# A streaming-encoder layer: two feature blocks half plain, their combinations on VectorE, taps on ScalarE, and a gate put into down weights

## The chip, the core and the metric

The kernel runs as one program on one core of a Trainium2 chip. The metric is the device time of a launch in microseconds; the table below gives three runs and one profiled execution. The engines are called TensorE (PE in the rows; PEld is its weight load), VectorE (DVE), ScalarE (ACT), GpSimd (POOL) and SyncE (SP, which issues nearly all transfers). All sums are in fp32; a matmul operand is split into a rounded part and a rest (hi and lo), and each product is three matmuls: hi x hi, hi x lo, lo x hi.

## What is computed

One layer of an encoder for 1024 prompt tokens and 8 x 16 sample tokens, 1152 in all. Ahead of the part in question lie the input projection, attention and retention. The rest, cut to what matters:

```python
x = x + gt_m * (mixed @ w_out)
h = rmsnorm(x, g_ffn) * (1.0 + sc_f) + sh_f
u = h @ w_up                                    # 1024 x 5632
ue = concatenate([conv_prev, u], axis=1)
y = sum(w_conv[j] * ue[:, j:j + L] for j in range(3)) + b_conv
a, g = split(y, 2)
x = x + gt_f * ((silu(a) * g) @ w_down)         # 2816 x 1024
y_out = rmsnorm(x, g_final)
```

`gt_f`, `sc_f` and `sh_f` come from a conditioning vector per sequence: one for the prompt, eight for the sample streams.

## The kernel before, in words

**Output projection** (`mains`, `merge`, `tail`). The tokens are nine tiles of 128, taken in the order 0, 4, 1, 5, 2, 6, 3, 7, 8; tile 8 holds the sample tokens. Each tile has two halves of 512 output columns, with weights of their own (`woh`, `wol`). `merge` multiplies by the gate on VectorE (`tm`) and adds x on GpSimd. `tail` norms the tile (`xn`), transposes it on TensorE (8 transposes), applies scale and shift on VectorE (`hfc`), stores it to the DRAM tensor `d_h`, and splits it into `hhi` and `hlo`, the matmul operands.

**Up projection** (`up`, one call for each of 22 feature blocks of 128 features `a` and 128 features `g`). The input is taken as 2 halves of h (kh) by 2 halves of the tokens (th, 576 each), and the product as seven products in place of eight, numbered 1 to 7, with combinations of weights (`up_first`, `up_rest`) and of tokens (`t_sets`: t5, t6, t7, and a combination that takes the place of part of `hhi`). A product is done in two chunks of 288 tokens (c = 0, 1), 12 matmuls each: 14 x 12 = 168 a block. Products 1, 6, 7 and 4 add up in one PSUM bank, which is read between them. `t_sets(c)` loads four pieces of `d_h` into buffers `y`, subtracts (VectorE and GpSimd, line 1223) and splits. It needs 576 tokens of each half, so all tiles of the order but, for c = 0, tiles 3, 7 and 8. In the kernel before, both sets are built behind the last `tail`.

`conv` makes the three taps of the width-3 convolution over the whole block row `U` on VectorE: one `tensor_scalar` (line 1263) and two `scalar_tensor_tensor` (line 1266); `a` then goes through SiLU on ScalarE, the two are multiplied (line 1329) and stored to `d_g`.

**Down projection.** The 22 blocks are taken in groups (`GROUPS`). For each group and each tile and half, TensorE sums the group's products into one bank; VectorE adds the bank to `facc` (line 1476). `entry` loads and splits the next group's rows of `d_g` and weights. In the group before the last ("pen"), `facc` is multiplied by the gate (line 1482) and x is added on GpSimd (line 1483); in the last group the sum of a bank is multiplied by the gate (line 1479) and added by GpSimd, or for tile 7 by VectorE (line 1480). `finish_rows` norms a tile and stores it.

**What sets the order.** TensorE's instructions stand in program order. A scheduler sets the order on the other engines; each engine then runs its list strictly in order, so an instruction that waits holds all behind it. SyncE's transfers are such a list too.

Of the kernel before, what the change touches and what calls it, by code (L numbers as in the profile page):

```python
# [15 lines left out]
D = 1024  # L16
# [23 lines left out]
GROUPS = (2, 4, 3, 4, 3, 3, 3)  # L40
# [7 lines left out]
def body(ctx: ExitStack, tc: tile.TileContext, i):  # L48
# [818 lines left out]
    def up_first(A, s1):  # L867
# [202 lines left out]
    with ExitStack() as st:  # L1070
        c2 = cp = st.enter_context(pool("cb"))
# [57 lines left out]
        def tail(t, xt):  # L1129
# [7 lines left out]
            for q in range(2):  # L1137
# [26 lines left out]
        for n in range(1, NT):  # L1164
# [23 lines left out]
        up_rest(A0, s10, W0)  # L1188
        tail(NT - 1, xs.pop(NT - 1))

    wo_st.close()
    tails = ctx.enter_context(pool("tl")).tile([128, 18, 44], F32, name="tails")
    fst = ExitStack()
    tx = fst.enter_context(pool("tx"))
    TT = {p: [tx.tile([128, 4, TH], F32R, name=f"t{p}{z_}") for z_ in "hl"] for p in (5, 6, 7)}
    fp = fst.enter_context(pool("f"))

    def ytile():
        return fp.tile([128, UW], F32, tag="y", bufs=4, name="y")
# [14 lines left out]
    def t_sets(c):  # L1214
# [15 lines left out]
        sub(G, b[0, 1], b[1, 1], b[0, 1])  # L1230
# [3 lines left out]
        sub(G, b[1, 0], b[1, 0], b[1, 1])  # L1234
        s4 = slice(TH + c * CW, TH + c * CW + CW)
        split(hhi[:, 0:4, s4], hlo[:, 0:4, s4], b[1, 0])

    def up(ft, W, order, mid=None):
        kts = [s_ * NFT + ft for s_ in range(2)]
        Us, ys, X, Y, p5 = [], {}, {}, {}, {}  # L1240
        for s_ in range(2):
            U = fp.tile([128, UW], F32, tag="U", bufs=2, name="U")
# [28 lines left out]
        def keep(s_):  # L1271
            G.tensor_copy(tails.rearrange("p (i j) k -> p i j k", j=2)[:, :, :, kts[s_]],
                          Us[s_][:, SEQ:].rearrange("p (i c) -> p i c", c=2)[:, 0::9])

        def post3(c):
            for o_, ps_ in second(0, c, Y[3, c]):
                V.tensor_tensor(out=o_, in0=o_, in1=ps_, op=ALU.add)

        nb_ = [0]
        seen = set()  # L1280
        for p, c in order:
# [4 lines left out]
            else:  # L1286
                Y[p, c] = bank(nb_[0] // 2)
                nb_[0] += 1
                o = Y[p, c][:, 0:CW]
# [7 lines left out]
            seen.add((p, c))  # L1297
# [285 lines left out]
```

## Time and profile before

| | us |
|---|---|
| three runs | 1600.34, 1606.54, 1608.24 (median 1606.54) |
| the profiled execution | 1601.77 |
| its span in the profile | 1599.9 |
| TensorE busy in it | 1524.6 |
| VectorE, ScalarE, GpSimd busy | 1019.3, 513.7, 421.5 |

A line of the profile gives an engine, a source line of the kernel, the operation, the tensor written and the tensors read, and shapes as partitions x elements. Times are microseconds unless marked ns. "idle before" is what the engine stood still ahead of an instruction, and the name behind the arrow is what ended it. PEclk is the granted clock of TensorE; 1.00 stands for 2.4 GHz and 0.5 for 1.2 GHz.

### The profile page before, as it was taken

What the parts mean: (1) busy time and instruction counts of PE and PEld (TensorE: products, weight loads), DVE (VectorE), ACT (ScalarE), POOL (GpSimd) and SP (SyncE); (2) the same over time, 40 slices, a digit from 0 to 9 for tenths busy, and PEclk for the clock granted to TensorE, in tenths of its full rate; (3) what the DMA queues carried; (4) which work ended last, traced back from release to release, by engine and by line L of the source; (5) the groups of instructions that cost most, each with busy time, mean ns of one, the idle gap of its engine ahead of it and who ended that gap; (6) DMA issues with size and microseconds to landing.
All of it is one profiled execution on the core that took longest, in us unless ns stands there. A gap on an engine that the chain in (4) does not pass through costs nothing.

```text
span 1599.9 us, 27087 instructions
## 1 busy us (share of the span) xinstructions
PE 1524.6 (95%) x10544; PEld 1382.9 (86%) x10544; DVE 1019.3 (64%) x1754; ACT 513.7 (32%) x1039; POOL 421.5 (26%) x443
## 2 busy tenths in 40 slices
PE   6999999999999999899679999999999999999996
PEld 5866999998998898788569999999999987888785
DVE  5711248888755335455687888888888865544456
ACT  5401125555322423332332333323333244212102
POOL 2000021210221004333344444444444310000065
PEclk9999999999999999999979999999999999999998
DMA  9865321213258477565422222222222236322022
GB/s 304 267 253 183 93 85 53 67 42 98 65 188 276 142 247 241 168 215 165 152 79 83 77 70 66 79 83 76 70 62 83 83 129 215 122 84 85 34 92 118
DMA packets 190315, 203.89 MB, mean 127 GB/s; under 512 B 11181, under 2 KB 149723, under 8 KB 190188
## 3 DMA queue, kind: packets, MB, share of 16 engines
q1 hardware_dynamic: 171212, 187.22, 36.1%
q10 hardware_dynamic: 18976, 14.95, 2.9%
q8 instruction: 83, 1.36, 0.4%
q14 instruction: 44, 0.36, 0.1%
HBM read 152.56 MB, written 49.56 MB: 126 GB/s over the span
## 4 chain that ended last, share of the span: by engine, by line
PE 81%; DVE 6%; DMA 5%; issue 3%; ACT 2%; SPq 1%; POOL 1%; POOLq 0%; ACTq 0%; DVEq 0%
PE dn L61 9%; PE dn L63 9%; PE dn L62 9%; PE pb L1295 6%; PE pb L1294 6%; PE pb L1296 6%; PE dn L1295 3%; PE dn L1296 3%; PE dn L1294 3%; PE pf L62 2%; PE pf L63 2%; PE pf L61 2%; PE tp L660 2%; PE sc L625 1%; PE pa L372 1%
## 5 line engine op out<-in xcount | busy, mean ns | idle before, releaser
L61 PE MATMUL dn<-w,hhi 128*128 128x256 f32 x648 | 190.6, 294 | 0.0
L63 PE MATMUL dn<-w,hlo 128*128 128x256 f32 x648 | 182.1, 281 | 0.0
L62 PE MATMUL dn<-w,hhi 128*128 128x256 f32 x648 | 181.8, 281 | 0.0
L1266 DVE SCALAR_TENSOR_TENSOR y<-U,cv,y 128x1168 f32<-128x1168 f32 x88 | 153.6, 1747 | 1.6
L61 PEld LDWEIGHTS dn<-w,hhi 128*128 128x128 f32 x648 | 123.0, 190 | 12.0 <-issue 10.2
L63 PEld LDWEIGHTS dn<-w,hlo 128*128 128x128 f32 x648 | 122.8, 190 | 7.5 <-issue 7.5
L62 PEld LDWEIGHTS dn<-w,hhi 128*128 128x128 f32 x648 | 123.0, 190 | 4.3 <-issue 4.2
L245 POOL TENSOR_TENSOR sg<-sg,rot 128x256 f32<-128x256 f32 x36 | 28.1, 782 | 275.1 <-DVE rot L244 233.6
L1483 POOL TENSOR_TENSOR facc<-facc,x 128x1024 f32<-128x1024 f32 x9 | 21.7, 2406 | 229.2 <-DVE facc L1482 229.2
L57 ACT CAST sl<-raw 128x512 fp32r<-128x512 f32 x66 | 39.0, 620 | 108.3 <-PE pb L1295 59.1
L57 ACT CAST se<-raw 128x512 fp32r<-128x512 f32 x66 | 41.1, 622 | 95.3 <-PE dn L1295 52.3
L61 PE MATMUL dn<-hhi,w 128*128 128x384 f32 x192 | 69.3, 361 | 0.0
L63 PE MATMUL dn<-hhi,w 128*128 128x384 f32 x192 | 64.6, 336 | 0.0
L62 PE MATMUL dn<-hlo,w 128*128 128x384 f32 x192 | 64.5, 336 | 0.0
L58 DVE TENSOR_TENSOR w<-raw,w 128x512 fp32r<-128x512 f32 x56 | 38.9, 709 | 37.3 <-ACT w L57 25.1
L878 POOL TENSOR_TENSOR raw<-s,raw 128x512 f32<-128x512 f32 x22 | 49.5, 2249 | 46.6 <-DVE se L58 46.5
L61 PE MATMUL dn<-woh,mh 128*128 128x512 f32 x144 | 58.7, 408 | 1.7 <-issue 1.2
L1294 PE MATMUL dn<-t5h,sl 128*128 128x288 f32 x168 | 51.1, 304 | 8.6 <-issue 5.6
L1295 PE MATMUL pb<-t6l,sl 128*128 128x288 f32 x176 | 53.4, 303 | 6.0 <-DVE t6l L58 6.0
L62 PE MATMUL dn<-wol,mh 128*128 128x512 f32 x144 | 56.9, 395 | 2.2 <-DVE wol L58 2.2
L1476 DVE TENSOR_TENSOR facc<-facc,pf 128x512 f32<-128x512 f32 x45 | 30.9, 686 | 43.4 <-PE pf L63 42.3
L631 ACT ACTIVATE e<-sc,sm 128x128 f32<-128x128 f32 (+7 forms) x64 | 47.4, 745 | 30.9 <-DVE sm L630 30.1
(395 smaller groups left out, 4979.1 us busy)
## 6 DMA issues: line engine op xcount, KB each, us to landing
wa<-in_w_ada SPq DMA_DIRECT2D x48, 512.0 KB
raw<-in_w_up SPq DMA_DIRECT2D x88, 256.0 KB
raw<-in_w_in SPq DMA_DIRECT2D x56, 256.0 KB
gr<-d_g SPq DMA_DIRECT2D x20, 576.0 KB
d_g<-y SPq DMA_DIRECT2D x22, 512.0 KB
wr<-in_w_down SPq DMA_DIRECT2D x40, 256.0 KB
kc<-in_cache_k SPq DMA_DIRECT2D x8, 1024.0 KB
vc<-in_cache_v SPq DMA_DIRECT2D x8, 1024.0 KB
```

What stands on the lines that cost most here:

```text
L57: S.copy(hi, src)
L58: V.tensor_tensor(out=lo, in0=src, in1=hi.bitcast(F32), op=ALU.subtract)
L61: T.matmul(out, lhsT=sh, rhs=mh, start=first, stop=False)
L62: T.matmul(out, lhsT=sh, rhs=ml, start=False, stop=False)
L63: T.matmul(out, lhsT=sl, rhs=mh, start=False, stop=last)
L631: S.activation(out=e[:, hf, 0:nk], in_=s_[:, 0:nk], func=ACTF.Exp, bias=sm[:, hf:hf + 1], scale=1.0, accum_out=sm[:, 2 + hf:3 + hf])
L660: T.matmul(po[:, 0:128], lhsT=pTs[n // 4][:, n % 4], rhs=vt[:, n], start=(n == 0), stop=(n == qb))
L878: G.tensor_tensor(out=A[0, 0], in0=s1, in1=A[0, 0], op=ALU.subtract)
L1266: V.scalar_tensor_tensor(out=y[:, j0:j1], in0=U[:, j0 + j:j1 + j], scalar=wconv[j][:, kt:kt + 1], in1=y[:, j0:j1], op0=ALU.mult, op1=ALU.add)
L1294: T.matmul(o, lhsT=sh, rhs=mh, start=st_, stop=False, skip_group_check=True)
L1295: T.matmul(o, lhsT=sh, rhs=ml, start=False, stop=False, skip_group_check=True)
L1296: T.matmul(o, lhsT=sl_, rhs=mh, start=False, stop=en, skip_group_check=True)
```

## The change

1. **Blocks 0 and 1 half plain** (`NPL = 2`). Chunk 0 goes as before, with seven products. Chunk 1 is done plain, as eight products (`block`, the entries "q" of the order): 96 matmuls in place of 84. These need no combination of tokens. `t_sets(1)` is called behind block 1.
2. **Hand-over.** In block 0, products 1 and 2 of chunk 0 and the first halves of both plain parts come first (72 matmuls); then `handover` calls the last `tail`, frees the projection's memory, and calls `t_sets(0)` and the weights of block 1.
3. **Combinations on VectorE.** All four of a block's weights, and all four of a token set.
4. **Taps on ScalarE.** The first tap, and the scale and shift of tiles 0 to 7 in `tail`.
5. **Last group.** The last tile of it, 8, is done inside the group before, with the weights as they are; then the last group's down weights are loaded again, multiplied by the prompt's gate and split, so that the bank's sum is simply added to `facc`. The groups are 2, 2, 4, 3, 4, 3, 4 in place of 2, 4, 3, 4, 3, 3, 3.

```diff
-GROUPS = (2, 4, 3, 4, 3, 3, 3)
+GROUPS = (2, 2, 4, 3, 4, 3, 4)
+NPL = 2
...
+        late(4, A[1, 1])
+        V.tensor_tensor(out=s1, in0=A[1, 0], in1=A[1, 1], op=ALU.add)
+        late(5, s1)
+        V.tensor_tensor(out=A[1, 0], in0=A[0, 0], in1=A[1, 0], op=ALU.subtract)
+        V.tensor_tensor(out=A[0, 0], in0=s1, in1=A[0, 0], op=ALU.subtract)
+        late(6, A[0, 0])
+        V.tensor_tensor(out=A[0, 1], in0=A[0, 1], in1=A[0, 0], op=ALU.subtract)
...
-                        V.tensor_scalar(out=hf_[:, kk], in0=p_[:, k], scalar1=A[:, kk, 0:1], scalar2=B[:, kk, 0:1],
-                                        op0=ALU.mult, op1=ALU.add)
+                        S.activation(out=hf_[:, kk], in_=p_[:, k], func=ACTF.Identity, scale=A[:, kk, 0:1],
+                                     bias=B[:, kk, 0:1])
...
-        sub(G, b[0, 1], b[1, 1], b[0, 1])
+        sub(V, b[0, 1], b[1, 1], b[0, 1])
...
-            V.tensor_scalar(out=y[:, j0:j1], in0=U[:, j0:j1], scalar1=wconv[0][:, kt:kt + 1],
-                            scalar2=bconv[:, kt:kt + 1], op0=ALU.mult, op1=ALU.add)
+            S.activation(out=y[:, j0:j1], in_=U[:, j0:j1], func=ACTF.Identity, scale=wconv[0][:, kt:kt + 1],
+                         bias=bconv[:, kt:kt + 1])
...
+    def handover():
+        tail(NT - 1, xs.pop(NT - 1))
+        cb_st.close()
+        wo_st.close()
...
+        t_sets(0)
+        late_["W"] = up_w(1)
...
-    t_sets(0)
-    t_sets(1)
-    W = up_w(1)
...
+    mixed = [(1, 0), (5, 0), (2, 0), ("q", 0), (6, 0), ("q", 1), (3, 0), ("q", 0), (7, 0), ("q", 1), (4, 0)]
+    up(0, W0, [(1, 0), (2, 0), ("q", 0), ("q", 1), ("q", 0), ("q", 1), (5, 0), (6, 0), (3, 0), (7, 0), (4, 0)],
+       (4, handover))
...
+            up(ft, W, mixed if ft < NPL else both)
+        if ft == NPL - 1:
+            t_sets(1)
...
+                if pen and n_ == 4:
+                    for hf in range(2):
+                        add(8, hf, sums(8, [ents[n] for n in range(starts[NG - 1], NFT)], hf))
+                    gated_rows(8)
+                    finish_rows(8, facc[8], gfin)
+                    for n in range(starts[NG - 1], NFT):
+                        for hf in range(2):
+                            sl = slice(hf * 512, hf * 512 + 512)
+                            raw = wraw()
+                            nc.sync.dma_start(raw, i["w_down"][n * 128:n * 128 + 128, sl])
+                            V.tensor_tensor(out=raw, in0=raw, in1=gts[0][:, sl], op=ALU.mult)
+                            split(*(z_[:, sl] for z_ in ents[n][1]), raw)
```

Two places of VectorE's list show what moves. The first is the end of the projection, from the last two products with the gate (`tm`) to the scale of tile 8 (`hfc` from `mA`); `y` is a piece of `d_h`, `sl` a weight's rest, `rstd` and `xn` the norm of tile 8. Before:

```order
L1121 TENSOR_TENSOR tm<-dn,gtm 128x512 x2
L1144 TENSOR_SCALAR hfc<-ct,mA_83,mB_85 128x128 x8
L58 TENSOR_TENSOR sl<-s_7932,sl 128x512
L130 TENSOR_SCALAR rstd<-ss 128x1
L58 TENSOR_TENSOR sl<-raw,sl 128x512
L1134 TENSOR_SCALAR xn<-xt,rstd 128x1024
```

And with the change:

```order
L1130 TENSOR_TENSOR tm<-dn,gtm 128x512
L1226 TENSOR_TENSOR y<-y 128x1152
L1130 TENSOR_TENSOR tm<-dn,gtm 128x512
L1226 TENSOR_TENSOR y<-y 128x1152 x2
L59 TENSOR_TENSOR hlo<-hfc,hhi 128x4x128
L1226 TENSOR_TENSOR y<-y 128x1152
L59 TENSOR_TENSOR sl<-raw,sl 128x512
L1338 TENSOR_TENSOR U<-U,dn 128x288
L131 TENSOR_SCALAR rstd<-ss 128x1
L59 TENSOR_TENSOR hlo<-hfc,hhi 128x4x128
L59 TENSOR_TENSOR sl<-s_7932,sl 128x512
L1143 TENSOR_SCALAR xn<-xt,rstd 128x1024
```

All four subtractions of the first token set, which used to stand behind tile 8, are now ahead of its norm, one of them ahead of its last product with the gate. Block 0's first results (`U`) are read there too.

The second is VectorE's list between blocks 1 and 2: block 1's second convolution (two L1271) and the second token set (L1226, then the rests t5l and t7l). With the change:

```order
L1271 SCALAR_TENSOR_TENSOR y<-U,cv,y 128x1168
L59 TENSOR_TENSOR sl<-raw,sl 128x512
L1271 SCALAR_TENSOR_TENSOR y<-U,cv,y 128x1168
L59 TENSOR_TENSOR se<-raw,se 128x512
L1226 TENSOR_TENSOR y<-y 128x1152
L1352 TENSOR_TENSOR y<-y 128x1024
L890 TENSOR_TENSOR raw<-s_9050,raw 128x512
L1226 TENSOR_TENSOR y<-y 128x1152
L1354 TENSOR_TENSOR y<-y 128x128
L59 TENSOR_TENSOR t5l<-y,t5h 128x4x288
L1226 TENSOR_TENSOR y<-y 128x1152
L59 TENSOR_TENSOR t7l<-y,t7h 128x4x288
```

The second set stands behind the convolution of block 1, and the product of block 1 (L1352, L1354) between its subtractions.

## Rows read from the trace of the kernel before

**Rows 1.** The page, part 2: busy tenths of TensorE in 40 slices of the span.
```profile
PE   6999999999999999899679999999999999999996
```
**Rows 2.** Windows: length; busy of PE, PEld, DVE, ACT, POOL; clock, DMA share, GB/s.
```profile
700.00:772.00 72.00, 72.00 (x346) 59.01 (x345) 38.85 (x83) 21.92 (x34) 23.33 (x22) 1.00 0.51 165
...
780.10:831.20 51.10, 31.98 (x171) 29.86 (x170) 40.54 (x51) 16.75 (x22) 21.91 (x15) 0.71 0.43 130
...
1000.00:1200.00 200.00, 200.00 (x1506) 199.78 (x1505) 172.04 (x231) 64.97 (x126) 94.78 (x90) 1.00 0.24 74
...
1320.00:1340.00 20.00, 17.61 (x67) 13.32 (x66) 13.47 (x17) 13.68 (x22) 0.00 (x0) 0.91 0.92 312
1340.00:1586.30 246.30, 246.21 (x1057) 196.78 (x1055) 129.78 (x170) 43.13 (x64) 44.53 (x30) 1.00 0.26 90
1586.30:1599.90 13.60, 0.00 (x0) 0.00 (x0) 7.71 (x10) 3.32 (x7) 3.30 (x6) 0.67 0.32 128
```
**Rows 3.** Waits of TensorE, 772 to 831.2 us: for whom, total, times, longest.
```profile
PE pb L1295 <- DVE t6l L58: 6.0, 2, 3.0
PE dn L1294 <- issue: 5.6, 1, 5.6
PE ct L1140 <- DVE xn L1134: 4.9, 1, 4.9
PE dn L1295 <- DVE t5l L58: 4.5, 2, 2.3
PE dn L1294 <- ACT t5h L57: 3.0, 1, 3.0
```
**Rows 4.** Timeline of VectorE around tile 8's tail: start, length, instruction.
```profile
767.29 0.69 DVE L1121 TENSOR_TENSOR tm<-dn,gtm 128x512 f32<-128x512 f32 x1 [0.83 <-PE dn L63]
772.79 0.69 DVE L1121 TENSOR_TENSOR tm<-dn,gtm 128x512 f32<-128x512 f32 x1 [4.80 <-PE dn L63]
...
777.67 0.75 DVE L1134 TENSOR_SCALAR xn<-xt,rstd 128x1024 f32<-128x1024 f32 x1
...
780.14 1.07 DVE L1148 TENSOR_TENSOR hfc<-ct,mA 128x128 f32<-128x128 f32 x5
...
793.69 1.36 DVE L1223 TENSOR_TENSOR y<-y 128x1152 f32<-128x1152 f32 x1 [1.01 <-DMA y<-d_h]
```
**Rows 5.** Timeline of TensorE between the projection and block 0.
```profile
772.59 1.03 PE L1140 MATMUL ct<-ident_all,xn 128*128 128x128 f32 x8
778.47 1.96 PE L1140 MATMUL ct<-ident_all,xn 128*128 128x128 f32 x8 [4.85 <-DVE xn L1134]
...
781.43 0.44 PE L1296 MATMUL pb<-hhi,se 128*128 128x288 f32 x1
781.67 0.41 PE L1294 MATMUL pb<-hhi,se 128*128 128x288 f32 x1
```
**Rows 6.** Timeline of SyncE: the loads of the first token set.
```profile
787.37 2.31 SPq L1219 DMA_DIRECT2D y<-d_h  x4
```
**Rows 7.** Groups of VectorE, 793 to 831 us: busy us, mean ns.
```profile
L58 DVE TENSOR_TENSOR t6l<-y,t6h 128x1152 fp32r<-128x1152 f32 x2 | 7.5, 3746 | 0.0
...
L1223 DVE TENSOR_TENSOR y<-y 128x1152 f32<-128x1152 f32 x4 | 5.4, 1349 | 1.0 <-DMA y<-d_h 1.0
L1266 DVE SCALAR_TENSOR_TENSOR y<-U,cv,y 128x1168 f32<-128x1168 f32 x2 | 2.9, 1430 | 0.0
```
**Rows 8.** Lines 1263 and 1269, all of the span: min/median/max ns, first and last start.
```profile
L1263 DVE TENSOR_SCALAR y<-U,cv x44: 875/880/1978, 824.9 to 1302.3; 128x1168 f32<-128x1168 f32 x44
...
L1269 ACT ACTIVATE y<-y x22: 1181/1182/1192, 829.0 to 1300.1; 128x1168 f32<-128x1168 f32 x22
```
**Rows 9.** Timeline of VectorE at the end.
```profile
1590.70 0.68 DVE L1479 TENSOR_TENSOR tm<-tp,gtf 128x512 f32<-128x512 f32 x1
...
1592.71 0.68 DVE L1480 TENSOR_TENSOR facc<-facc,tm 128x512 f32<-128x512 f32 x1
```
**Rows 10.** GpSimd in the group before the last, 1510 to 1550 us: busy us, mean ns.
```profile
L1483 POOL TENSOR_TENSOR facc<-facc,x 128x1024 f32<-128x1024 f32 x8 | 19.2, 2404 | 227.4 <-DVE facc L1482 227.4
```

More of the change, by code (lines that the diff above doesn't have):

```diff
@@ L1271, in keep, with done, block @@
         def keep(s_):
-            G.tensor_copy(tails.rearrange("p (i j) k -> p i j k", j=2)[:, :, :, kts[s_]],
+            G.tensor_copy(late_["tails"].rearrange("p (i j) k -> p i j k", j=2)[:, :, :, kts[s_]],
                           Us[s_][:, SEQ:].rearrange("p (i c) -> p i c", c=2)[:, 0::9])
[L1275 to L1281, printed above, removed]
+        def done(s_, th, c):
+            have.add((s_, th, c))
+            if th and c:
+                keep(s_)
+            if len([z_ for z_ in have if z_[0] == s_]) == 4:
+                conv(s_, 0, YW)
+        nb_ = nbank
+        have = set()
+        def block(s_, c):
+            for th in range(2):
+                o = bank(nb_[0] // 2)[:, 0:CW]
+                nb_[0] += 1
+                for kh in range(2):
+                    for k in range(4):
+                        cs = slice(th * TH + c * CW, th * TH + c * CW + CW)
+                        kk = kh * 4 + k
+                        mm3(o, *(z_[:, k] for z_ in W[((1, 2), (0, 4))[s_][kh]]), hhi[:, kk, cs], hlo[:, kk, cs],
+                            kk == 0, kk == 7)
+                if th:
+                    for o_, ps_ in second(s_, c, o):
+                        S.copy(o_, ps_)
+                else:
+                    S.copy(Us[s_][:, 2 + c * CW:2 + c * CW + CW], o)
+                done(s_, th, c)
+                yield
+        blocks = [block(s_, 1) for s_ in range(2)]
+        for n_, (p, c) in enumerate(order):
+            if mid and mid[0] == n_:
+                mid[1]()
+            if p == "q":
+                next(blocks[c])
+                continue
             if p in (1, 6, 7, 4):
@@ L1313, in up @@
                     V.tensor_tensor(out=o_, in0=ps_, in1=q_, op=ALU.add)
[L1314 to L1315 removed]
+                done(1, 1, c)
             elif p == 3:
[L1317 to L1318 removed]
+                for o_, ps_ in second(0, c, o):
+                    V.tensor_tensor(out=o_, in0=o_, in1=ps_, op=ALU.add)
+                done(0, 1, c)
             else:
                 S.copy(Us[1][:, f0], o)
[L1321 to L1327 removed]
+                done(1, 0, c)
         ya, yg = ys[0], ys[1]
@@ L1370, in body @@
         if last:
-            up(ft, W, [(p, c) for p in (1, 2, 5, 6, 3, 7, 4) for c in range(2)], ((3, 1), early))
+            up(ft, W, [(p, c) for p in (1, 2, 5, 6, 3, 7, 4) for c in range(2)], (10, early))
         else:
-            up(ft, W, both)
+            up(ft, W, mixed if ft < NPL else both)
+        if ft == NPL - 1:
+            t_sets(1)
         W = Wn
@@ L1448, in finish_rows, with sums, add, gated_rows @@
             nc.sync.dma_start(y_out, f)
-        for g in range(len(GROUPS)):
-            es = [ents.pop(n) for n in range(starts[g], starts[g + 1])]
-            pen, last = g == len(GROUPS) - 2, g == len(GROUPS) - 1
+        def sums(t, es, hf):
+            tk, sl = slice(t * 128, (t + 1) * 128), slice(hf * 512, hf * 512 + 512)
+            p_ = dbank()
+            for n, (g_, w_) in enumerate(es):
+                mm3(p_, g_[0][:, tk], g_[1][:, tk], w_[0][:, sl], w_[1][:, sl], n == 0, n == len(es) - 1)
+            return p_
+        def add(t, hf, p_):
+            sl = slice(hf * 512, hf * 512 + 512)
+            V.tensor_tensor(out=facc[t][:, sl], in0=facc[t][:, sl], in1=p_, op=ALU.add)
+        def gated_rows(t):
+            x1 = f2.tile([128, D], F32, tag="x1", bufs=2, name="x1")
+            nc.sync.dma_start(x1, d_x1[t * 128:(t + 1) * 128])
+            V.tensor_tensor(out=facc[t], in0=facc[t], in1=gts[t == 8], op=ALU.mult)
+            G.tensor_tensor(out=facc[t], in0=facc[t], in1=x1, op=ALU.add)
+        NG = len(GROUPS)
+        for g in range(NG):
+            es = [ents[n] for n in range(starts[g], starts[g + 1])]
+            pen, last = g == NG - 2, g == NG - 1
             if not last:
@@ L1468, in body @@
                 for hf in range(2):
[L1469 to L1472 removed]
+                    p_ = sums(t, es, hf)
                     if g == 0:
[L1474 to L1480 removed]
```

113 lines of the change are left out of this document (42 added, 71 removed).

## The prediction

> **What bounds the kernel now.** I read the page first: TensorE is busy 1524.6 of 1599.9 us, and its slices fall furthest below 9 in the first, in the 20th and 21st (760 to 840 us) and in the last [rows 1]. The stretches say the same in microseconds [rows 2]. In 700 to 772 us (output projection) and in 1000 to 1200 us (feature blocks in steady state) TensorE has no idle time at clock 1.00. 1506 matmuls in 200 us make **0.1328 us a matmul**, so a block of 168 takes 22.3 us. Block 0, from 780.1 to 831.2 us, takes 51.1 us, with 32.0 busy, at a mean granted clock of 0.71: 28.8 us lost. Smaller losses are 2.4 us idle and a clock of 0.91 in 1320 to 1340, and 13.6 us behind TensorE's last matmul.
>
> Third, the waits of TensorE in the hand-over [rows 3]: it waits for xn of the last tile (4.9 us), then twice for each of t5h, t5l and t6l, the combinations built on VectorE and GpSimd from d_h. Two sets, so two series of waits, and behind each the clock is at 1.2 GHz. Everything in the change that matters happens there or in the last 50 us; in between, TensorE is the bound.
>
> **The change part by part.** *Hand-over, block 0.* The order of TensorE now puts 72 matmuls that need no late tile (half of the plain work) between the projection and tile 8's transposes. The projection's last bank is read at 772.79 [rows 4]; eight transposes take 1.03 [rows 5], so TensorE is at about 773.6, and 72 x 0.1328 = 9.6 us bring it to 783.2, tile 8's transposes to 784.2. Before, it waited 4.9 us here.
>
> VectorE now has the first combination set ahead of, and between, the steps of tile 8 (first pair of excerpts of its order). The four loads of d_h can go out once the first half's output weights are free, which the read of that bank at 767.29 marks [rows 4]. Before, the loads went out from 787.37 [rows 6] and the first subtraction began at 793.69 [rows 4], 6.3 us later; so the first subtraction comes at about 773.6 and ends at 774.9, and tile 8's multiplication behind it is 2.1 us later than at 772.79. From there to xn the old queue took 5.6 us (772.79 to 778.4). The new one holds three more subtractions of 1.35 [rows 7], two of the third and fourth load, and some splits: I get xn at 782.8, a split of 1.3 and three of 0.7 behind it, then the 16 tile-8 operations (five took 1.07: 3.3 us), two casts and two splits. The operands of tile 8 are there at about 790.8, and TensorE waits **6.6 us** from 784.2. When TensorE resumed at 778.47 behind 4.9 us of idleness, its matmuls were 0.24 apart up to 781.67 [rows 5], against 0.133 in steady state: 3.2 us at the lower level (1.2 GHz) cost about 1.5. So the remaining 48 plain matmuls end at 790.8 + 6.4 + 1.5 = 798.7. The casts of t5 to t7 and their splits (1.35) run during these, without a GpSimd subtraction beside them, beside which the t6l split took 3.75, a subtraction of the same shape 1.35 [rows 7]. The last 60 matmuls take 8.0, and I add 0.8 for (4,0), which follows (7,0) at once and needs its sum read first. Block 0 ends at 807.5 instead of 831.2: **-23.7 us**.
>
> *Block 1* has 180 matmuls instead of 168: +1.6 us.
>
> *Block 2* is the first that needs the second set, which now stands on VectorE behind block 1's convolution (third excerpt). Block 1 ends at 831.5. Copy and tap on ScalarE take 1.6; then two taps of 1.4, splits, two subtractions of 1.35, the product of 1.2 and the t5l split come to 9.7 us: t5l at 842.9. TensorE reaches (5,1) after 36 matmuls, at 836.3. It waits **6.6 us**, pays 1.5 at 1.2 GHz, and waits about 1.4 for t6l, which is held by the fourth load (its buffer is free only after block 1's product is stored): +9.5 us. A row for this place does not exist. The bounds are nothing (the set finished in block 1's slack) and 14 us (it stalls as the second set did before: 3.0 + 2.2 + 3.0 [rows 3], and some 50 matmuls at 1.2 GHz cost 5.5). I take the reckoned 9.5, nearer to those rows.
>
> *Steady state, blocks 3 to 21.* The first tap leaves VectorE (0.88) for ScalarE, where a pass of the same shape takes 1.18 [rows 8]; four weight combinations of 512 elements come to VectorE from GpSimd, 0.68 each by the addition of that shape [rows 9]. VectorE: 2 x 0.88 off, 4 x 0.68 on, +1.0 us a block. It goes from 0.86 [rows 2] to 0.90 at most, less as far as GpSimd no longer holds it up; ScalarE from 0.32 to about 0.43; TensorE at 100% covers both: 0. If the cover were gone, 1 us a block would be 19 us. The eight hfc passes of a tile, moved to ScalarE, lie under a projection with no idle time: 0.
>
> *Down projection, start.* Group 1 has two entries instead of four, so its loads and splits fit into group 0. TensorE stands idle there for 2.4 us, and 20 us at a clock of 0.91 lose another 1.8 [rows 2]. I take **-3.5** of these 4.2; the bounds are 0 and -4.2.
>
> *Last two groups.* Gated weights replace a product and a GpSimd addition per half tile by one addition. TensorE ends at 1586.3 [rows 2]; the last half tile's product starts only at 1590.70 and its sum ends at 1593.4 [rows 9], behind products, GpSimd additions and scalings in a queue. Now the sum ends one addition (0.68) behind TensorE, at +0.7 instead of +7.1: **-6.4**. In return the penultimate group carries eight more loads (2 MB, hidden at a DMA share of 0.26), eight products and eight splits. Behind tile 8's early finish VectorE has 15.6 us of work until the last weights are split, and TensorE needs them 18.5 us on (four tiles of 18 matmuls and 9 more, 246.2/1057 = 0.233 each [rows 2]). Alone it would fit: 0. But GpSimd adds x to facc with 2.40 us each, five times in that stretch [rows 10], and the t6l split shows what that can do [rows 7]. Full exclusion would make 15.6 + 12.0 - 18.5 = 9.1 us late, 10.7 with the clock. The products from PSUM, half of that work, kept 0.68 at the end, where GpSimd adds too [rows 9], so I take a third: **+3**.
>
> **Sum:** -23.7 + 1.6 + 9.5 - 3.5 - 6.4 + 3.0 = -19.5 us on the profiled execution, 1601.77 to 1582.3. That execution lies low among the runs shown (1600.34, 1606.54, 1608.24); the mean of all four is 1604.2, so I give **1585**.
>
> **Two rules of the Trainium skill.** "SBUF — State Buffer", section "SBUF: two separate sides", states that VectorE with two SBUF inputs and GpSimd hold one port pair as an exclusive lock, for a whole instruction. The t6l rows agree. By the rule the +3 would be +10.7 and the sum 7.7 us more; this is rival 3. "ScalarE: Activation LUTs", "Rules for kernel authors", says to use VectorE, not ScalarE, for add and mul, so it speaks against the moved taps. The rows agree on the price (1.18 against 0.88), and by it the sum would change only where a tap is waited for, 0.3 us at the last block; it would matter in rival 4.
>
> **Rivals.**
> 1. *Both late sets are hidden.* VectorE's queue drains earlier than I count, block 2 does not wait and the last group starts on time: 1585 - 9.5 - 3 = 1572. For: VectorE no longer shares with GpSimd. Against: the second set stands behind block 1's last tap in program order.
> 2. *The early loads are late.* They leave behind the store of tile 3 and beside the loads of x and w_up. If they land 8 us later, VectorE stands at its first subtraction with tile 8's product behind it, and TensorE runs out of plain work: +8, 1593; with the second set delayed as well, 1600.
> 3. *The lock decides in the penultimate group*: 1585 + 7.7 = 1593.
> 4. *Slower: the convolution chain of every block becomes the bound.* Place: VectorE's queue between one block's last tap and the next block's read of (6,0), 8.0 us into the block by my count; TensorE needs that read at 96 matmuls, 12.8 us. It decides once ScalarE's tap and the combinations delay the queue by over 4.8 us. One microsecond beyond costs 1 + 1.5 of clock in each of 19 blocks, 48 us: about 1633. Against it: by the sum above VectorE stays at or below 0.90.
>
> **How the numbers follow.** Chances: forecast 0.52, rival 1 0.15, rival 2 0.18, rival 3 0.10, rival 4 0.05. About 0.5% (8 us, 1598.5) is what a measurement of this kernel can tell. All of the forecast and rival 1, most of rivals 2 and 3, are faster: 0.82; the far end of rival 2 and two errors together are the same: 0.12; slower 0.06. The range 1570 to 1599 takes in rival 1 and rival 2's far end.
>
> **What would show it.** In the new profile: no wait for xn right behind the projection; one wait of 4 to 9 us for tile 8's hhi or hlo near 785 to 791; no t5 or t6 wait in block 0; one wait of about 7 us for t5l one block and a half later; no idle time in steady state; at most a microsecond of idle time in the first two groups of the down projection; 7 us instead of 13.6 behind the last matmul. The forecast is wrong if VectorE stands waiting for y before tile 8's product for over 4 us, or if TensorE shows gaps in blocks 3 to 21.

## The result and the profile after

Four runs of the changed kernel: 1575.91 to 1579.30 us, median **1576.56**; the kernel before: 1600.34 to 1608.24, median 1604.58. The ratio is 0.983, 95% interval 0.980 to 0.986. The forecast was 1585, the range 1570 to 1599. The profiled execution took 1576.79 us (before: 1601.77), its span is 1575.0 us (before: 1599.9).

The page, part 2, of the changed kernel:

```profile
PE   6999999999999999999897999999999999999998
```

The hole at 760 to 840 us has shrunk to an 8 in the slice from 748 to 788 us, a 7 stands at 827 to 866 us, and the last slice has risen from 6 to 8. Windows of the same trace (length; busy of PE, PEld, DVE, ACT, POOL; clock, DMA share, GB/s), cut at the projection's last matmul (770.07), the ends of blocks 0, 1 and 2, and so on:

```profile
770.07:806.10 36.03, 29.48 (x198) 28.45 (x197) 31.26 (x52) 20.64 (x39) 5.88 (x8) 0.86 0.37 118
...
829.93:864.83 34.90, 25.06 (x170) 24.28 (x169) 26.91 (x38) 14.54 (x20) 9.97 (x6) 0.85 0.40 123
...
1000.00:1200.00 200.00, 200.00 (x1515) 200.00 (x1514) 157.54 (x253) 89.41 (x145) 24.64 (x54) 1.00 0.24 75
1287.04:1338.00 50.96, 50.43 (x226) 41.20 (x225) 35.56 (x46) 29.55 (x47) 0.00 (x0) 1.00 0.68 235
...
1478.00:1486.00 8.00, 7.69 (x24) 5.61 (x25) 4.76 (x6) 5.05 (x8) 0.00 (x0) 0.79 0.78 269
1568.06:1575.00 6.94, 0.00 (x1) 0.00 (x0) 2.29 (x4) 1.44 (x3) 0.74 (x2) 0.82 0.39 151
```

The waits of TensorE in blocks 0 to 2 (for whom; total, times, longest), which answer to [rows 3]:

```profile
PE tp L1325 <- ACT t5h L58: 6.7, 1, 6.7
PE tp L62 <- ACT hhi L58: 5.0, 1, 5.0
PE tp L1326 <- DVE t5l L59: 2.7, 1, 2.7
PE tp L63 <- DVE hlo L59: 0.8, 1, 0.8
PE pb L1325 <- DVE U L1342: 0.6, 1, 0.6
PE pb L1326 <- DVE t6l L59: 0.5, 1, 0.5
PE ct L1149 <- DVE xn L1143: 0.2, 1, 0.2
```

`hhi` and `hlo` are tile 8's, in block 0; t5 and t6 are those of the second set, in block 2. The forecast term by term, from where blocks begin and end in the two timelines of TensorE (a block runs from its first matmul to the next block's first):

| stretch | before | after | change | forecast |
|---|---|---|---|---|
| to the projection's last matmul | 772.6 | 770.1 | -2.5 | 0 |
| from there to the end of block 0 | 58.6 | 36.0 | -22.6 | -23.7 |
| block 1 | 22.3 | 23.8 | +1.5 | +1.6 |
| block 2 | 22.3 | 34.9 | +12.6 | +9.5 |
| blocks 3 to 21 | 22.34 each | 22.22 each | -2.2 | 0 |
| down projection to the last matmul | 285.8 | 280.9 | -5.0 | -0.5 |
| behind the last matmul | 13.8 | 7.1 | -6.7 | -6.4 |
| sum | 1599.9 | 1575.0 | -24.9 | -19.5 |

So over half of what the new hand-over gains in block 0 is given back in block 2.

### The profile page after: what moved, and what is told of

The parts are those of the page before. It is cut to its first block, busy times and chain, and to the rows that moved or that the text cites. A ratio compares the mean times of both kernels' runs of the same rounds, so it can differ in the third digit from the quotient of the medians.

```text
span 1575.0 us, 27021 instructions
## 1 busy us (share of the span) xinstructions
PE 1519.5 (96%) x10568; PEld 1381.3 (88%) x10568; DVE 971.9 (62%) x1743; ACT 602.8 (38%) x1166; POOL 232.7 (15%) x335
## 4 chain that ended last, share of the span: by engine, by line
PE 85%; DVE 6%; DMA 5%; ACT 2%; issue 1%; SPq 1%; POOL 0%; ACTq 0%; POOLq 0%; DVEq 0%
PE dn L62 10%; PE dn L63 9%; PE dn L64 9%; PE pb L1325 5%; PE pb L1326 5%; PE pb L1327 5%; PE pf L64 3%; PE pf L63 3%; PE pf L62 3%; PE dn L1325 2%; PE dn L1327 2%; PE dn L1326 2%; PE tp L1325 2%; PE tp L1327 2%; PE tp L1326 2%; PE tp L63 2%
## 5 line engine op out<-in xcount | busy, mean ns | idle before, releaser
L1271 DVE SCALAR_TENSOR_TENSOR y<-U,cv,y 128x1168 f32<-128x1168 f32 x88 | 124.4, 1431 | 3.0 <-ACT y L1268 2.1
L58 ACT CAST sl<-raw 128x512 fp32r<-128x512 f32 x68 | 42.2, 622 | 110.7 <-PE pb L1326 101.9
L1277 POOL COPY tails<-U 128x18 f32<-128x18 f32 x44 | 21.4, 487 | 283.2 <-DVE U L1342 192.4
L1268 ACT ACTIVATE y<-U,cv 128x1168 f32<-128x1168 f32 x44 | 60.1, 1367 | 4.6 <-DVE U L1346 0.5
L59 DVE TENSOR_TENSOR w<-raw,w 128x512 fp32r<-128x512 f32 x56 | 39.1, 712 | 35.8 <-ACT w L58 23.6
L1493 DVE TENSOR_TENSOR facc<-facc,pf 128x512 f32<-128x512 f32 x54 | 36.9, 683 | 39.1 <-PE pf L64 39.1
L64 PE MATMUL dn<-woh,ml 128*128 128x512 f32 x144 | 57.0, 396 | 0.0
L58 ACT CAST ew<-wr 128x512 fp32r<-128x512 f32 x24 | 14.5, 619 | 109.6 <-PE tp L63 85.7
```

Source lines behind the costliest of these rows:

```text
L58: S.copy(hi, src)
L59: V.tensor_tensor(out=lo, in0=src, in1=hi.bitcast(F32), op=ALU.subtract)
L64: T.matmul(out, lhsT=sl, rhs=mh, start=False, stop=last)
L1268: S.activation(out=y[:, j0:j1], in_=U[:, j0:j1], func=ACTF.Identity, scale=wconv[0][:, kt:kt + 1], bias=bconv[:, kt:kt + 1])
L1271: V.scalar_tensor_tensor(out=y[:, j0:j1], in0=U[:, j0 + j:j1 + j], scalar=wconv[j][:, kt:kt + 1], in1=y[:, j0:j1], op0=ALU.mult, op1=ALU.add)
L1493: V.tensor_tensor(out=facc[t][:, sl], in0=facc[t][:, sl], in1=p_, op=ALU.add)
```

## Experiments

All of them in one table: median of all runs, ratio to the kernel before with its interval, then from the profiled execution the end of the projection, blocks 0, 1, 2, the mean of the later ones, the down projection and what lies behind it (us).

| kernel | median | ratio (95%) | ends | 0 | 1 | 2 | later | down | behind |
|---|---|---|---|---|---|---|---|---|---|
| before | 1604.58 | 1 | 772.6 | 58.6 | 22.3 | 22.3 | 22.34 | 285.8 | 13.8 |
| before2 | 1610.38 (one run) | | 776.6 | 59.6 | 22.3 | 22.3 | 22.34 | 289.4 | 13.8 |
| changed | 1576.56 | 0.983 (0.980 to 0.986) | 770.1 | 36.0 | 23.8 | 34.9 | 22.22 | 280.9 | 7.1 |
| after2 | 1580.57 | 0.984 (0.981 to 0.986) | 773.5 | 35.9 | 23.8 | 34.8 | 22.26 | 280.9 | 7.1 |
| a_oldend | 1594.61 | 0.993 (0.991 to 0.996) | 775.2 | 36.3 | 23.8 | 34.1 | 22.22 | 290.2 | 13.5 |
| p_late | 1578.30 | 0.983 (0.979 to 0.986) | 769.8 | 35.7 | 23.8 | 35.0 | 22.26 | 282.5 | 7.1 |
| d_noplain | 1576.91 | 0.983 (0.980 to 0.986) | 771.0 | 47.7 | 22.2 | 22.2 | 22.22 | 282.4 | 7.1 |
| b_gps | 1583.74 | 0.987 (0.984 to 0.989) | 773.4 | 38.0 | 23.9 | 35.5 | 22.22 | 282.7 | 7.1 |
| c_taps | 1590.24 | 0.991 (0.989 to 0.993) | 772.1 | 38.0 | 23.9 | 34.1 | 22.55 | 283.6 | 7.1 |
| bc_undo | 1589.06 | 0.990 (0.988 to 0.992) | 773.3 | 39.3 | 24.6 | 36.6 | 22.23 | 284.6 | 7.1 |
| e_mid | 1569.48 | 0.978 (0.975 to 0.980) | 775.4 | 35.8 | 23.8 | 22.2 | 22.22 | 282.6 | 7.1 |
| f_npl3 | 1567.90 | 0.978 (0.975 to 0.980) | 768.8 | 35.9 | 23.9 | 23.8 | 22.22 | 282.3 | 7.1 |
| k_best | 1565.81 | 0.975 (0.973 to 0.977) | 776.7 | 36.0 | 23.8 | 22.2 | 22.22 | 277.8 | 7.1 |
| n_best | 1564.90 | 0.975 (0.973 to 0.977) | 770.0 | 36.9 | 23.9 | 22.8 | 22.26 | 277.9 | 7.1 |

The column "down" needs care. One and the same down projection takes 280.9 us in the changed kernel and in after2, and 282.3 to 282.7 in d_noplain, b_gps, e_mid and f_npl3. The difference is the granted clock behind the gate's matmuls: over 8 us there it is 0.79 in the changed kernel (second window from the end, above), which loses 1.7 us, and 0.57 in e_mid, which loses 3.4:

```profile
1470.00:1478.00 8.00, 7.07 (x15) 4.20 (x15) 5.25 (x6) 5.89 (x9) 0.00 (x0) 0.57 0.77 277
```

The kernel before has two such levels as well, 285.8 and 289.4 us (before2). So the -5.0 of the sum is -8.5 against before2, and a difference of 2 us in this column shows nothing of an edit by itself.

**after2: how much an execution moves by itself.** No edit.

> The changed kernel, unchanged, on another chip. Its projection ended at 770.07 us in the profile shown, and at 768.8 to 775.4 in the kernels derived from it, which do the same up to there. If that is the luck of an execution, it lies in that span here too, with block 0 at 36.0 us, block 2 at 34.9 and 19 blocks of 22.22. 1574 to 1580.

The projection ended at 773.5 us, with the rest as before but for one wait of 0.4 us in the later blocks; the median, 1580.57, is just above what was expected. The change leaves alone all that TensorE does up to there, and the column "ends" spreads from 768.8 to 776.7. So a single profile moves by some 8 us there, and the -2.5 us of the first row of the sum are no effect of the change. I compare stretches, and medians only with their intervals.

**a_oldend: without the new last groups.** The down projection and GROUPS of the kernel before, the rest changed.

```diff
-GROUPS = (2, 2, 4, 3, 4, 3, 4)
+GROUPS = (2, 4, 3, 4, 3, 3, 3)
...
+                        V.tensor_tensor(out=tm, in0=p_, in1=gt[:, sl], op=ALU.mult)
+                        (V if t == 7 else G).tensor_tensor(out=f[:, sl], in0=f[:, sl], in1=tm, op=ALU.add)
```

> The changed kernel with the groups, the last two groups and the gate of the kernel before. Theory 1 (the two traces add up part by part: the down projection gives 5.0 us between its first and last matmul and 6.6 us behind the last one): these 11.6 us come back, 1576.6 + 11.6 = about 1588. Rival (only the tail behind the last matmul belongs to the gate; the 5.0 us come from a GpSimd that does less everywhere): about 1583, with the first group's idle time absent still.

6.4 us come back behind the last matmul and 9.3 ahead of it, 15.7 together, more than theory 1 said. The first group's waits are back (0.7, 0.7, 0.6 and two more), with a mean clock of 0.76 over 14 us, where [rows 2] have 0.91 over 20, and behind the gate's matmuls the clock is 0.55:

```profile
1316.00:1330.00 14.00, 11.69 (x36) 8.18 (x36) 10.32 (x12) 9.88 (x15) 0.00 (x0) 0.76 0.84 288
1503.00:1510.00 7.00, 7.00 (x16) 4.37 (x15) 1.10 (x2) 0.77 (x2) 0.00 (x0) 0.55 0.00 0
```

14 us lose 2.3 by waiting and 3.4 by the clock here, and 7 us lose 3.2. GpSimd has nothing to do in either stretch, so the rival is out. The 5.7 us of the first stretch are the groups' own. The 3.2 behind the gate's matmuls are not: the changed kernel loses 1.7 at that place, and e_mid, with the same ending, 3.4.

**p_late: the margin in the group before the last.** Tile 8's last sums and the new weights one tile later.

```diff
-                if pen and n_ == 4:
+                if pen and n_ == 5:
```

> The changed kernel with tile 8's last sums and the new gated weights one tile later in the group before the last. In the changed kernel TensorE came to the last group at 1523.4 us and its last split weight was there at 1524.8, for a matmul at about 1525.5. Theory 1 (the margin is that thin): one tile later, 4.2 us, TensorE waits 3 to 5 us in all at the start of the last group, and the kernel is that much longer. Rival (VectorE had room and would merely do these steps in another order): no wait above 1 us, same time.

TensorE waited 1.3 us for a split weight, and the down projection was 1.6 us longer, between the two theories, with the clock behind the gate's matmuls as in the changed kernel (0.79 over 8 us):

```profile
1527.56 0.50 PE L63 MATMUL pf<-hlo,hhi 128*128 128x512 f32 x1 [1.28 <-DVE hlo L59]
```

The room was not the 0.7 us of the expectation, which set the wrong split against that matmul. The split that ends at 1524.9 in the changed kernel is the second half's, and TensorE reads it at 1528.5 only. The first half's ended at 1523.7 and its matmul stood at 1525.7 (both lines are shown below, at the last weights): a room of 2.1 us. In p_late it ended at 1527.5, 1.4 us behind the time at which its matmul was due.

**d_noplain: are the plain halves worth anything?** The new hand-over, early loads and engines, but both token sets in block 0 and no plain half.

```diff
-NPL = 2
+NPL = 0
...
         t_sets(0)
+        t_sets(1)
...
-    up(0, W0, [(1, 0), (2, 0), ("q", 0), ("q", 1), ("q", 0), ("q", 1), (5, 0), (6, 0), (3, 0), (7, 0), (4, 0)],
+    up(0, W0, [(1, 0), (1, 1), (2, 0), (2, 1), (3, 0), (3, 1), (5, 0), (6, 0), (5, 1), (6, 1),
+               (7, 0), (7, 1), (4, 0), (4, 1)],
```

> The changed kernel without plain halves: both chunks of every block as seven products, both token sets in the hand-over, in the new order of the hand-over (48 matmuls that need no late tile, then tile 8, then product 3). The three first blocks take 103.3 us behind the projection before and 94.8 changed. Theory 1 (the plain halves are what fills TensorE): a wait for t5, t6 of either set as before, block 0 near 52 us, three blocks 97, 1579 or more. Rival (the early loads and VectorE's order are what helps, and the stall of block 2 eats what the plain halves gain): block 0 near 45 us, three blocks 90, 1572 or less.

The three blocks took 92.2 us, against 94.8 with plain halves and 103.3 before; the time is the same, since in this profile the down projection took 1.5 us more and the projection ended 0.9 later. Both theories missed the size (block 0 47.7, foreseen 52 or 45), and the rival's point stands: as built, the plain halves gain 11.7 us in block 0 and cost 1.6 in block 1 and 12.7 in block 2.

**e_mid: the place of the second set.** Its loads, subtractions and splits of t5 to t7 inside block 1; behind block 1 only the split that replaces part of `hhi`, which block 1's plain half still reads.

```diff
-            up(ft, W, mixed if ft < NPL else both)
+            up(ft, W, mixed if ft < NPL else both, (3, lambda: t_sets(1, 0)) if ft == 1 else None)
         if ft == NPL - 1:
-            t_sets(1)
+            t_sets(1, 1)
```

> The changed kernel with the second token set's loads, subtractions and splits of t5, t6 and t7 called inside block 1, and only the split that replaces a part of hhi behind block 1. On VectorE's list the subtractions stand ahead of block 1's convolution instead of behind it. Theory 1 (block 2 takes 34.9 us instead of 22.2 because of that place in the list): t5h and t5l are there in time, block 2 takes 22 to 25 us, 1564 to 1568. Rival (VectorE's own work in blocks 1 and 2, 17 + 11 us and 17 us against 46 us of TensorE, leaves no room): the wait turns into one for a read of the bank in block 1 or 2, blocks 1 and 2 together above 54 us, 1572 or more.

Block 2 takes 22.2 us. The three blocks take 81.9 instead of 94.8, and the waits of TensorE in them are those of block 0 alone:

```profile
PE tp L62 <- ACT hhi L58: 5.0, 1, 5.0
PE tp L63 <- DVE hlo L59: 0.8, 1, 0.8
PE pb L1330 <- DVE U L1347: 0.6, 1, 0.6
PE ct L1149 <- DVE xn L1143: 0.4, 1, 0.4
```

The rival was near: VectorE is busy 22.85 of block 1's 23.84 us, and it just fits. Theory 1 is shown by the block's length; the median fell by less than 12.7 us (1569.48), with a projection that ended 5.4 us later and a down projection 1.7 us longer in this profile.

**f_npl3: a whole block more for it.** Three blocks half plain, the set called at the end of block 1, its replacing split behind block 2.

```diff
-NPL = 2
+NPL = 3
```

> The changed kernel with three blocks half plain, the second token set called near the end of block 1, its replacing split behind block 2. Theory 1: the same set has a whole block more, so no wait in blocks 1 to 3; block 2 takes 23.8 us (180 matmuls), block 3 takes 22.2: 1576.6 - 12.7 + 1.6 = 1566. Rival (VectorE full): a wait in block 2 or 3 of over 5 us, 1571 or more.

No wait in blocks 1 to 3, block 2 at 23.8 us: as theory 1 said, and the same time as e_mid within the intervals. The third plain block is not needed.

**b_gps: combinations back on GpSimd.**

```diff
-        V.tensor_tensor(out=s1, in0=A[1, 0], in1=A[1, 1], op=ALU.add)
+        G.tensor_tensor(out=s1, in0=A[1, 0], in1=A[1, 1], op=ALU.add)
...
-        sub(V, b[0, 1], b[1, 1], b[0, 1])
+        sub(G, b[0, 1], b[1, 1], b[0, 1])
```

> The changed kernel with the four weight combinations of a block and two of the four token subtractions back on GpSimd. Theory 1 (matmuls of the steady state stand 0.1322 us apart instead of 0.1329 because GpSimd is quiet, 2.2 us over 19 blocks, and VectorE's splits in the hand-over are no longer held up): spacing back to 0.1329 and +2 us, with up to 5 us more where a split stands beside a GpSimd subtraction: 1579 to 1584. Rival (the spacing differs from execution to execution and the combinations are hidden on either engine): 1576 to 1578, spacing 0.1322.

Blocks stay at 22.22 us, so a quiet GpSimd is not what makes the matmuls stand closer. The three blocks lose 2.7 us, the largest new wait being 2.5 us for a weight's rest in block 0. The medians are 7.2 us apart; in this profile 3.3 lie ahead of the change and 1.8 in the down projection. What GpSimd costs VectorE stands in VectorE's groups from 1000 to 1200 us (busy us, mean ns | idle before); of the changed kernel:

```profile
L1271 DVE SCALAR_TENSOR_TENSOR y<-U,cv,y 128x1168 f32<-128x1168 f32 x36 | 50.7, 1430 | 0.3
L59 DVE TENSOR_TENSOR sl<-raw,sl 128x512 fp32r<-128x512 f32 x28 | 19.3, 690 | 0.0
...
L59 DVE TENSOR_TENSOR sl<-s,sl 128x512 fp32r<-128x512 f32 x9 | 6.1, 678 | 0.0
```

and of b_gps:

```profile
L1271 DVE SCALAR_TENSOR_TENSOR y<-U,cv,y 128x1168 f32<-128x1168 f32 x36 | 57.8, 1625 | 6.5 <-ACT y L1268 6.1
L59 DVE TENSOR_TENSOR sl<-raw,sl 128x512 fp32r<-128x512 f32 x27 | 24.2, 895 | 0.2
...
L59 DVE TENSOR_TENSOR sl<-s,sl 128x512 fp32r<-128x512 f32 x9 | 15.9, 1767 | 0.0
```

**c_taps: first tap, scale and shift back on VectorE.**

```diff
-            S.activation(out=y[:, j0:j1], in_=U[:, j0:j1], func=ACTF.Identity, scale=wconv[0][:, kt:kt + 1],
-                         bias=bconv[:, kt:kt + 1])
+            V.tensor_scalar(out=y[:, j0:j1], in0=U[:, j0:j1], scalar1=wconv[0][:, kt:kt + 1],
+                            scalar2=bconv[:, kt:kt + 1], op0=ALU.mult, op1=ALU.add)
```

> The changed kernel with the first tap and the scale and shift of tiles 0 to 7 back on VectorE. Theory 1 (both hidden on either engine): 1575 to 1578, TensorE without idle time in the steady state. Rival (VectorE's queue in the hand-over is what TensorE waits for, so every pass put back there is paid: eight small ones of the tile before, two taps in block 1): the waits for tile 8 and for t5h grow by 1 to 4 us, 1578 to 1582.

Neither: the price lies in the steady state. Each block takes 22.55 us, 19 x 0.33 = 6.2 us in all; the hand-over adds 1.2. The place is product 6, which goes into the bank that product 1 left. TensorE's timeline of one block (start, length):

```profile
1032.70 0.29 PE L1327 MATMUL tp<-t5h,sl 128*128 128x288 f32 x1
1033.10 0.40 PE L1325 MATMUL pb<-t6h,sl 128*128 128x288 f32 x1
1033.35 0.30 PE L1326 MATMUL pb<-t6l,sl 128*128 128x288 f32 x1
```

0.40 and 0.25 us stand where 0.13 each is usual, and 17 of the later blocks have such a gap. ScalarE's timeline says why:

```profile
1031.58 1.18 ACT L1274 ACTIVATE y<-y 128x1168 f32<-128x1168 f32 x1 [1.19 <-DVE y L1271]
1032.67 0.68 ACT L1330 COPY U<-pb 128x288 f32<-128x288 f32 x2
```

Its read of the bank (line 1330) stands behind the SiLU of the block before, and the SiLU waits for VectorE's last tap, which the first taps have made late. With the taps on ScalarE the same place shows a single wait of 0.4 to 0.6 us in after2, p_late and n_best and none in the other profiles, so the room there is thin. The profile is 12.1 us longer than that of the changed kernel; what is not named yet, 4.7 us, is the projection's 2.0 and the down projection's 2.7.

**bc_undo: both engine moves undone.** The two edits above together.

> The changed kernel with both engine moves undone: combinations on GpSimd and first tap, scale and shift on VectorE. Alone they cost 7 and 14 us. Theory 1 (with the taps back, VectorE has too much work in a block only because it has the combinations as well; 0.3 us in every block at the bank of products 1 and 6): without the combinations that gap all but goes, blocks of 22.22 to 22.34 us, and the whole is 1583 to 1588, less than the two added up (1597). Rival (the tap's instruction on VectorE slows TensorE by itself): blocks of 22.5 us again, 1593 or more.

Blocks of 22.23 us: the gap is gone without the combinations, so theory 1 holds for the blocks, and the rival is out. The hand-over pays instead: the three blocks take 100.5 us, 5.7 more than in the changed kernel, with 3.3 us for xn, 3.4 for tile 8 and 8.6 + 3.2 for t5. The time (1589) is that of c_taps alone, 1 us above theory 1's.

**before2: the blocks of 22.34.** No edit.

> The kernel before, unchanged, profiled on this chip. Its blocks took 22.34 us in the profile shown, those of the changed kernel 22.22. If that is in the kernel, they take 22.3 us here too; if it belongs to that execution, 22.22. Time about 1605.

22.34 us again, 1506 matmuls in 200 us, against 1515 in the changed kernel and 1514 in bc_undo, which has both engine moves undone:

```profile
1000.00:1200.00 200.00, 200.00 (x1506) 199.78 (x1505) 172.25 (x233) 64.01 (x124) 91.92 (x90) 1.00 0.24 75
```

So the 2.2 us belong to the kernel and not to an execution, and the engine moves are not their cause. What else differs inside a block (where buffers lie, a fifth buffer `y`, the order in which sums are read) was not tried; this stays open.

**k_best: tile 8 and the gate.** e_mid, with tile 8's transposes behind 48 matmuls, three subtractions put behind its norm, and the gate's eight matmuls in two parts.

```diff
-       (4, handover))
+       (3, handover))
...
+            with tc.issue_after(xn8[0].ins):
+                rest()
...
-                gts = [gate_f(0), gate_f(1)]
+                gts = [gate_f(0), None]
...
+                if pen and n_ == 2:
+                    gts[1] = gate_f(1)
```

> The second token set inside block 1 (e_mid), and two more edits. First: tile 8's transposes one entry earlier (behind 48 matmuls instead of 72), with all but the first subtraction of the first set, and its splits, put behind tile 8's norm on VectorE. Theory 1 (TensorE waits 5.8 us for tile 8 because VectorE does subtractions and splits first): the wait falls to 1 to 3 us and block 0 from 36.0 to 30 to 33. Rival (the chain behind the projection itself is that long): block 0 stays at 35 to 36. Second: the gate's eight matmuls split in two fours, two tiles apart. If their length in one piece makes the clock fall to 1.2 GHz behind them (about ten matmuls at 0.42 instead of 0.23 us in all profiles of the changed kernels), that piece shrinks and 1 to 2 us come off the down projection. In all 1561 to 1566.

Block 0 did not move, but for a reason that the rival does not give: VectorE still had a subtraction and three splits between the norm and the scales. Its timeline, without the splits:

```profile
783.79 0.75 DVE L1145 TENSOR_SCALAR xn<-xt,rstd 128x1024 f32<-128x1024 f32 x1
784.45 1.35 DVE L1235 TENSOR_TENSOR y<-y 128x1152 f32<-128x1152 f32 x1
...
787.53 1.47 DVE L1161 TENSOR_TENSOR hfc<-ct,mA 128x128 f32<-128x128 f32 x7
```

The gate's part held. Behind each four matmuls the granted clock stays at 1.00:

```profile
1470.40:1478.00 7.60, 7.60 (x34) 6.24 (x34) 7.04 (x10) 3.84 (x7) 0.00 (x0) 1.00 0.78 267
1484.00:1492.00 8.00, 8.00 (x37) 6.64 (x36) 7.93 (x8) 1.08 (x2) 5.55 (x2) 1.00 0.21 67
```

and the down projection takes 277.8 us: 3.1 less than in the changed kernel and 4.8 less than in e_mid, where the clock behind the one piece loses 1.7 and 3.4 us.

**n_best: tile 8 first on VectorE.** k_best, with the remaining subtractions and all of block 0's late weights but one behind tile 8's last scale.

```diff
-            with tc.issue_after(xn8[0].ins):
+            with tc.issue_after(late_h[0].ins):
                 rest()
...
+        with tc.issue_after(late_h[0].ins):
+            up_rest(A0, s10, W0, put0, True, 2)
```

> In k_best block 0 stayed at 35.95 us: VectorE still did a subtraction and three splits between tile 8's norm and its first scale, and another subtraction among the scales (its first scale came 3.1 us after the norm, the sixteen took 5.8 us instead of 3.3). Here all of that stands behind tile 8's last scale: three subtractions of the first token set with their splits, and all of block 0's weight combinations and rests but one. Theory 1 (the wait for tile 8 is VectorE's list): TensorE waits at most 2 us there, block 0 takes 30 to 33 us, 1560 to 1564. Rival (VectorE's whole work in block 0 is the limit, so what is put back is waited for later: t5, t6 or a weight's rest): the wait for tile 8 falls, but new ones take its place, block 0 35 us or more, 1566 or more.

The rival holds for block 0, though the time is 1 us below its 1566. The waits of TensorE in block 0, the longest first:

```profile
PE pb L1348 <- DVE sl L59: 2.1, 1, 2.1
PE tp L65 <- DVE hlo L59: 2.0, 1, 2.0
PE pb L1346 <- DVE U L1363: 1.3, 1, 1.3
PE pb L1347 <- DVE t6l L59: 1.1, 1, 1.1
PE tp L64 <- ACT hhi L58: 1.0, 1, 1.0
```

Tile 8's wait fell from 5.9 to 3.0 us, and a weight's rest, a bank's sum and t6l are waited for in its place; block 0 is 36.9. In this order VectorE only changes what is late. With 0.975 of the time before, k_best and n_best have the lowest ratios here; they cannot be told apart, and their intervals touch those of e_mid and f_npl3.

## Why the prediction was right, and where it was not

The sign and the range held. The step is larger than forecast, 24.9 us between the profiles (28.0 between the medians) in place of 19.5. Point by point:

- **Block 0, -23.7: measured -22.6.** The transposes ended at 781.9 (forecast 784.2 on a projection that ended 2.5 us later), the wait for tile 8 was 5.0 + 0.8 us (6.6), the matmuls behind it 0.24 apart, and no t5 or t6 was waited for. The mechanism is as told. That this gain is due to the plain halves is not: d_noplain has half of it without them. One sign that was named for a wrong forecast did come: VectorE stood over 4 us waiting for y ahead of tile 8's product.

```profile
770.39 1.36 DVE L1226 TENSOR_TENSOR y<-y 128x1152 f32<-128x1152 f32 x1 [4.14 <-DMA y<-d_h]
771.67 0.68 DVE L1130 TENSOR_TENSOR tm<-dn,gtm 128x512 f32<-128x512 f32 x1
```

 The sign was badly chosen. The product could not have started before TensorE's last matmul of the projection (770.07), and before the change VectorE stood 4.8 us at this place, waiting for TensorE [rows 4]; the early subtraction makes the product 1.3 us late, not 4.
- **Block 2, +9.5: measured +12.6.** The right wait at the right place, mis-sized by 3.1 us. The step that failed is "then two taps of 1.4, splits, two subtractions": it has no wait for a load, and the first subtraction came 9.0 us into block 2, where that list puts it at about 6. Two combinations of weights stand among the taps, and the first of them waited 3.12 us, with all taps and the second set behind it. VectorE's timeline in the changed kernel:

```profile
833.70 0.69 DVE L887 TENSOR_TENSOR s<-raw 128x512 f32<-128x512 f32 x1 [3.12 <-DMA raw<-in_w_up]
834.43 0.69 DVE L889 TENSOR_TENSOR raw<-raw 128x512 f32<-128x512 f32 x1
835.04 1.43 DVE L1271 SCALAR_TENSOR_TENSOR y<-U,cv,y 128x1168 f32<-128x1168 f32 x1
...
838.93 1.35 DVE L1226 TENSOR_TENSOR y<-y 128x1152 f32<-128x1152 f32 x1
...
843.41 1.35 DVE L59 TENSOR_TENSOR t5l<-y,t5h 128x1152 fp32r<-128x1152 f32 x1
```

 But this wait is worth only about 1 us of the 3.1. In c_taps it is 0.18 us and in a_oldend 1.28, and VectorE then stands idle in front of the first subtraction, 1.80 and 0.79 us, which comes 8.0 us into block 2 in both; block 2 takes 34.1 us, 0.8 less than here. In c_taps:

```profile
835.44 0.74 DVE L887 TENSOR_TENSOR s<-raw 128x512 f32<-128x512 f32 x1 [0.18 <-DMA raw<-in_w_up]
...
841.93 1.36 DVE L1226 TENSOR_TENSOR y<-y 128x1152 f32<-128x1152 f32 x1 [1.80 <-issue]
```

 The profile names nothing that ended this second wait. The loads of the two pieces of `d_h` that the subtraction reads had gone out 7.6 and 7.0 us before, so their landing is the likely cause, which is not shown. With the combinations on GpSimd (b_gps) the wait for the weights is GpSimd's, 3.15 us, and block 2 took 35.5 us all the same.
- **Steady state, 0: measured -2.2**, not foreseen and not explained (before2). VectorE's share went the other way from the forecast's "0.90 at most": 157.5 of 200 us instead of 172.0 [rows 2]. Two taps a block have left it, and what it took over from GpSimd costs it nothing more, since GpSimd no longer lengthens its passes (b_gps). Rival 4 named the right bank, though its wait runs over ScalarE; it comes true, at 0.3 us a block instead of 2.5, if the taps go back (c_taps). So the taps on ScalarE are what makes room for the combinations on VectorE.
- **Last weights, +3: measured 0.** The last split ended 17.8 us behind tile 8's last sums (1524.9 against 1507.1), where 15.6 was reckoned for VectorE alone and a wait of 3 us needs 21.5. Exclusion is there, but smaller than the share taken: behind those sums one split took 2.29 us and one product with the gate 2.09, both beside a GpSimd addition, 0.68 each alone. Three of the eight products had been done by 1491.2. And the matmul in question reads the first half's split (1523.0 + 0.7), which was there 2.1 us ahead of it. VectorE and TensorE:

```profile
1514.22 2.29 DVE L59 TENSOR_TENSOR ew<-wr,ew 128x512 fp32r<-128x512 f32 x1
...
1520.37 2.09 DVE L1533 TENSOR_TENSOR wr<-wr,gtf 128x512 f32<-128x512 f32 x1 [0.26 <-DMA wr<-in_w_down]
...
1522.99 0.68 DVE L59 TENSOR_TENSOR hlo<-wr,hhi 128x512 fp32r<-128x512 f32 x1
...
1524.19 0.68 DVE L59 TENSOR_TENSOR hlo<-wr,hhi 128x512 fp32r<-128x512 f32 x1
...
1525.73 0.39 PE L63 MATMUL pf<-hlo,hhi 128*128 128x512 f32 x1
```

- **Down projection's start, -3.5: the loss is gone**, nearly all of the 4.2 us of the bound: 0.5 us of idle time in its first 51 us at clock 1.00, against 3.0 us at 0.97 in the kernel before. On the other side stands a loss that I did not foresee, the clock of 0.79 behind the gate's matmuls, 8.0 x 0.21 = 1.7 us. The rest of the -5.0 was not followed.
- **End, -6.4: measured -6.7.**

The sum was 5.4 us off: +1.1 (block 0), +3.1 (block 2), -2.2 (steady state), -4.5 (down projection), -0.4 in the two small terms, and -2.5 us ahead of the change. The misses have both signs, and the last of them is the luck of an execution.

The Trainium skill, "SBUF — State Buffer", section "SBUF: two separate sides", has the port pair that VectorE and GpSimd share held by one of them for a whole instruction. b_gps agrees: with 24.5 us of combinations taken off VectorE (36 of 0.68), its busy time in 200 us stays at 157.8, as the three groups shown grow by 7.1 (taps), 5.5 (27 x 0.205) and 9.8 us (splits). The Trainium skill, "ScalarE: Activation LUTs", section "Rules for kernel authors", prefers VectorE for add and mul; c_taps disagrees here, where following it makes a block 0.33 us longer, though the pass itself is shorter (0.88 against 1.37 us).

## What to carry to other kernels

When work is moved out of a crowded hand-over, ask where it now stands in the queue of the engine that makes it: the plain halves gained 11.7 us in block 0 and lost 14.3 in the next two blocks, until the second set was called one block earlier. Here, combinations on GpSimd cost VectorE as much as doing them itself; but before they moved to VectorE, something else had to leave, and the wait for their load came with them, in front of all that stood behind (3.1 us once, of which about 1 us was paid). Compare stretches of two traces rather than their ends, since the shared beginning alone moved by 8 us from one execution to the next.

## What I had not expected of the hardware

The granted clock fell without an idle TensorE. Behind the gate's eight matmuls of 32 rows in one piece, some ten matmuls of 512 columns stood 0.43 us apart instead of 0.23, at the lower level of 1.2 GHz, in 11 of the 12 profiles with that piece. In the changed kernel 0.5 us of waiting lies within the piece, but in before2 and a_oldend there is none, and the clock fell at its seventh matmul. In the first profile of the kernel before, the same piece left the clock at 1.00. The piece in before and in before2:

```profile
1506.65 4.39 PE L1392 MATMUL tp<-ada,ident_all 32*128 32x512 f32 x8
1512.38 5.34 PE L1392 MATMUL tp<-ada,ident_all 32*128 32x512 f32 x8
```

Two pieces of four left the clock at 2.4 GHz in both kernels that have them (k_best, n_best).
